# Attention scores and recurrence gates: pairs of 64-row matmuls in place of stacked 128-row ones, in a hybrid decoder layer on one core

## The chip, the cores and the metric

The kernel runs on one core of a Trainium2 chip, as one launch. The metric is the time of an execution on the device in microseconds (us); lower is better. The core's engines work side by side, each through its own instructions in order: TensorE (PE, with its weight loads listed apart as PEld), VectorE (DVE), ScalarE (ACT), GpSimd (POOL) and SyncE (SP), which issues most transfers. They wait for one another through semaphores. Matrix products land in PSUM, in eight banks of 128 partitions by 512 floats; all else lies in SBUF.

## What is computed

One layer of a hybrid decoder over 16 learned meta tokens and 1024 tokens of width 1024, in float32. Cut to what matters here:

```python
u = rmsnorm(h)                       # 1040 x 1024
z = u @ w_in                         # -> q (8 heads of 64), k, v (2 heads of 64), x_rec, y_rec (512 each)
# sliding-window attention, blocks of 128 queries against their own and the previous block of keys
s = einsum("qd,sd->qs", q_block, keys_256) * 64 ** -0.5      # for each head
p = softmax over s and a sink of the head; o = p @ v
# recurrence on x = conv4(x_rec), gates from 8 blocks of 64 channels
r = sigmoid(x_block @ w_a[block] + b_a)
i = sigmoid(x_block @ w_x[block] + b_x)
a = exp(-8 * r * softplus(-lam));  h_t = a_t * h_(t-1) + sqrt(1 - a_t**2) * i_t * x_t
h += rmsnorm(concat(o, gelu(y_rec) * h_rec) @ w_out)
h += rmsnorm(relu(rmsnorm(h) @ w_ff1) ** 2 @ w_ff2)
```

The two contractions that the change touches, the scores and the gates, are over 64 values each.

## The kernel before, in words

**Precision.** Every product of float32 matrices is made of single-pass products of split operands: each operand is a high part (a rounded copy, type fp32r) and a low part (the rest). `mm3` (L123) adds three matmuls into one bank: high x high, high x low, low x high. `split` (L94) makes the parts: ACT casts (L96), DVE subtracts (L99). The one matmul operand is loaded into the array as weights, a row of the array for each value of the contraction; the other one streams past, a column for each result.

**Stages.** First the tokens are normed, transposed and split, in four pieces of 272 and 256 tokens; each piece is projected to k, v, the first pair of query heads and the first chunk of x_rec (L430 to L459). Then come eight rounds of attention: four pairs j of query heads (head j on the first key head, head j + 4 on the second), two halves of four query blocks each (L702 to L714). Each round calls `scores`, then `next_fill`, a projection of the next q, x_rec or y_rec piece that is given a late priority so that it fills gaps, and `attend` of the round before. Then the gates of four chunks of 128 channels (`gates`, L731), two more projections of y_rec, the recurrence (`decay`, `recur`, `rec_out`), the output projection and the feed-forward part. The order within each engine comes from a scheduler with its own estimates; `behind` (L106) and `chained` (L286) fix some orders by hand, and `lut` keeps ACT's table functions in the order of the program.

**Scores.** A head has 64 values, half of the array's rows. The kernel fills the other half with the low part: q[h] (L400) holds the high part of the head's queries in one half of its 128 partitions and the low part in the other, and khh[h] (L264) holds the high part of the keys in both. One matmul of q[h] with khh[h] gives (high + low) x high; a second one, with kl[h], whose other half is zero, gives high x low. So a score product takes two 128-row matmuls (L555 and L559). The sinks that build this, `sink_k` (L376) and `sink_q` (L404), take two ACT and two DVE instructions of 64 partitions each for every piece, and four transfers on POOL's queue copy the high keys to the other half (L462, and L463 for the meta keys in km). A round works head by head; for each head it fills two banks tagged "s" in turn, two blocks of queries each. ACT copies half of a bank (L573) and DVE overwrites what lies above the diagonal (L574).

**Gates.** A chunk has 128 channels, two blocks of 64. Their weights are put into graw as a block-diagonal 128x128 matrix on a zeroed tile (L717 to L724), so that one 128-row `mm3` computes one gate for both blocks. A chunk takes two gates, three pieces of 348 or 344 tokens and three matmuls each: 18, and 72 in all. Each result goes through a sigmoid (L745) into a tile whose 128 partitions are the chunk's channels, as the recurrence needs them.

Of the kernel before, what the change touches and what calls it, by code (L numbers as in the profile page):

```python
# [10 lines left out]
F32R = mybir.dt.float32r  # L11
AF = mybir.ActivationFunctionType
# [25 lines left out]
def hybrid_layer(  # L38
# [30 lines left out]
    def f32(ap):  # L69
        return ap.bitcast(F32)  # L70
# [189 lines left out]
    REAL2 = [(16, 512), (528, 512)]  # L260

    khh = [slot("b", [P, T], F32R) for _ in range(2)]  # L264
    kl = [slot("b", [P, T], F32R) for _ in range(2)]
    HALF = (slice(0, HD), slice(HD, P))
    for h in range(2):
        nc.gpsimd.memset(f32(kl[h][HALF[1 - h]]), 0.0)

    zero = slot("ws", [P, 512])  # L270
    nc.vector.memset(zero, 0.0)
    km = const.tile([P, 4, P], F32R, name="km")
    vm = const.tile([P, 2, P], F32R, name="vm")
    nc.vector.tensor_copy(km.rearrange("p a b -> p (a b)"), zero)

# [81 lines left out]
    for i, src in enumerate((conv_b, b_a, b_x, lru_lambda)):  # L357
        nc.sync.dma_start(prm_r[4 + i : 5 + i, :], src)


    vk = [slot("b", [P, 8, P], F32R) for _ in range(2)]
    vt = slot("c", [P, TT])


    def high_k(hh, src):
        return [nc.scalar.copy(hh[h][HALF[h]], src[HALF[h]]).ins for h in range(2)]

    def low_k(hh, lo, src):
        return [
            nc.vector.tensor_tensor(  # L370
                lo[h][HALF[h]], src[HALF[h]], f32(hh[h][HALF[h]]), op=ALU.subtract
            ).ins
            for h in range(2)
        ]

    def sink_k(acc, t0, n):  # L376
        o = NMETA if t0 == 0 else 0
        c = slice(t0 + o - NMETA, t0 - NMETA + n)
        parts = [([khh[0][:, c], khh[1][:, c]], [kl[0][:, c], kl[1][:, c]], acc[:, o:])]
        if o:  # L380
            m, mk = slice(0, NMETA), slice(P - NMETA, P)
            parts.append(
                ([km[:, 0, mk], km[:, 1, mk]], [km[:, 2, mk], km[:, 3, mk]], acc[:, m])
            )
        ops = [[], []]
        for hh, lo, src in parts:
            ops[0] += high_k(hh, src)
        for hh, lo, src in parts:
            ops[1] += low_k(hh, lo, src)
        if o:  # L390
            for e in range(2):
                for ins in ops[e]:
                    chained(e, ins)

    def sink_v(acc, t0, n):
# [4 lines left out]
    def new_q():  # L400

        q = pair("b", [P, T])

        def sink_q(acc, t0, n):  # L404
            c = slice(t0 - NMETA, t0 - NMETA + n)
            for h in range(2):
                r = HALF[h]
                nc.scalar.activation(q[h][r, c], acc[r], AF.Copy, scale=-(HD ** -0.5))
            for h in range(2):
                r, o = HALF[h], HALF[1 - h]  # L410
                nc.vector.scalar_tensor_tensor(
                    q[h][o, c], acc[r], -(HD ** -0.5), f32(q[h][r, c]),
                    op0=ALU.mult, op1=ALU.subtract,
                )

        return q, sink_q

# [12 lines left out]
    for b in range(4):  # L430
# [29 lines left out]
    for h in range(2):  # L460
        r, o, m = HALF[h], HALF[1 - h], slice(P - NMETA, P)
        nc.gpsimd.dma_start(f32(khh[h][o]), f32(khh[h][r]))  # L462
# [76 lines left out]
    def scores(j, half, q):  # L539

        sn = slot("c", [P, 2, 4, P + 1])
        negm = small.tile([P, 2, 4], F32, name="negm", tag="negm")
        den = small.tile([P, 2, 4], F32, name="den", tag="den")
        rden = small.tile([P, 2, 4], F32, name="rden", tag="rden")
        for h in range(2):
            nc.gpsimd.tensor_copy(
                sn[:, h, :, P], nsink[:, j + 4 * h : j + 4 * h + 1].to_broadcast([P, 4])
            )
        for h in range(2):
            for bp in range(2):  # L550
                sp_ = bank("s", (P, 2, 256))

                def qk(dst, b, hi, lo):
                    c = slice(b * P, (b + 1) * P)
                    nc.tensor.matmul(  # L555
                        dst, q[h][:, c], hi, start=True, stop=False,
                        skip_group_check=True,
                    )
                    nc.tensor.matmul(  # L559
                        dst, q[h][:, c], lo, start=False, stop=True,  # L560
                        skip_group_check=True,
                    )

                for i in range(2):
                    b = 4 * half + 2 * bp + i
                    if b == 0:
                        qk(sp_[:, i, 0:P], b, km[:, h, :], km[:, 2 + h, :])
                        qk(sp_[:, i, P:256], b, khh[h][:, 0:P], kl[h][:, 0:P])
                    else:
                        c = slice((b - 1) * P, (b + 1) * P)  # L570
                        qk(sp_[:, i, :], b, khh[h][:, c], kl[h][:, c])
                s_ = sn[:, h, 2 * bp : 2 * bp + 2, 0:P]
                nc.scalar.copy(s_, sp_[:, :, P:256])  # L573
                nc.vector.copy_predicated(  # L574
                    s_, above_i.rearrange("p (a b) -> p a b", a=1).to_broadcast([P, 2, P]),
                    sp_[:, :, 0:P],
                )
                if half == 0 and bp == 0:
                    w = slice(0, P - NMETA)
                    nc.vector.copy_predicated(sn[:, h, 0, w], above_i[:, w], far)  # L580
            nc.vector.tensor_reduce(
                negm[:, h, :], sn[:, h], axis=mybir.AxisListType.X, op=ALU.min
            )
# [68 lines left out]
            )  # L652
        xc[c] = y

    ys = [None] * NLRU

    def fill_q(j):
        def run(w):
# [11 lines left out]

    def fill_y(c):
        def run(w):
            y = slot("b" if c == 1 else "d", [P, T])

            def sink(acc, t0, n):
                nc.vector.tensor_copy(y[:, t0 - NMETA : t0 - NMETA + n], acc)

            project(w, REAL2, sink)
            ys[c] = y
        return run  # L680
# [22 lines left out]
    for j in range(NPAIR):  # L703
        for half in range(2):
            if j % 2 == 0 and half == 0:
                at_pair(j // 2)
            sn = scores(j, half, qs[j])
            if True:
                with deferred(FILL_LAG):
                    next_fill()  # L710
            if prev is not None:
                attend(*prev)
            prev = (j, half, sn)
    attend(*prev)  # L714


    graw = slot("e", [P, 2, NLRU, P])  # L717
    behind(last_pow[0], nc.gpsimd.memset(graw, 0.0).ins)
    for i, w in enumerate((w_a, w_x)):
        for s in range(2):  # L720
            r = slice(HD * s, HD * s + HD)
            nc.sync.dma_start(
                graw[r, i, :, r], w[0, s::2].rearrange("n c d -> c n d")
            )  # L724
    gh = slot("e", [P, 2, NLRU, P], F32R)
    gl = slot("b", [P, 2, NLRU, P], F32R)
    split(gh, gl, graw)

    rg = [None] * NLRU

    def gates(c):  # L731
        ch, cl = pair("b", [P, TT])
        split(ch, cl, xc[c])
        rg[c] = []
        for i in range(2):
            t_ = slot("c", [P, TT])
            for t0, n in ((0, 348), (348, 348), (696, 344)):
                flip[0] += 1
                acc = bank(("s", "pt", "o")[flip[0] % 3])
                mm3(  # L740
                    acc[:, :n], (gh[:, i, c, :], gl[:, i, c, :]),
                    (ch[:, t0 : t0 + n], cl[:, t0 : t0 + n]), True, True,
                )
                lut(
                    t_[:, t0 : t0 + n], acc[:, :n], AF.Sigmoid,  # L745
                    bias=prm[:, c, 5 + i : 6 + i],
                )
            rg[c].append(t_)
        nc.vector.tensor_tensor(t_, t_, xc[c], op=ALU.mult)

    av = [None] * NLRU

# [4 lines left out]
        lut(r, r, AF.Tanh, scale=m4sp[:, c : c + 1])  # L757

    def recur(c):
        r, gi = rg[c]  # L760
        lut(r, r, AF.Sqrt, scale=-1.0)
        nc.vector.scalar_tensor_tensor(r, av[c], 1.0, r, op0=ALU.add, op1=ALU.mult)
        nc.vector.tensor_tensor(gi, gi, r, op=ALU.mult)
# [640 lines left out]
```

## Time and profile before

| | us |
|---|---|
| median of 3 runs (lowest, highest) | 969.04 (965.6, 969.07) |
| the profiled execution, its own time | 966.98 |
| its span, first to last instruction | 965.3 |

The granted TensorE clock of that execution was 0.998 of full. By stages, in us from the start of the span:

| stage | from | to | matmuls |
|---|---|---|---|
| loads, norm, first piece | 0 | 22 | 80 |
| other pieces of k, v, first q and x_rec | 22 | 62 | 337 |
| attention and most filling projections | 62 | 201.5 | 953 |
| gates, with projections of y_rec among them | 201.5 | 220.4 | 106 |
| recurrence, beside the last projections and the output projection | 220.4 | 270 | 214 |
| rest of the output projection, feed-forward | 270 | 965.3 | 3036 |

How to read the rows below. A row of a group gives its line, engine and operation, the tile written and those read, and the shape. A row of the timeline gives start and duration in us. Matmuls are pipelined: the end of one is modelled, and what counts is how far their starts stand apart. "64x512" on ACT or DVE means 64 partitions with 512 values each; the time goes with the 512. In the list of waits stand the engine and line that waited, who ended the wait, the total in us, the number of times, and the longest.

### The profile page before, as it was taken

How to read it: one execution, taken by the hardware profiler on the slowest of the kernel's cores; microseconds unless marked ns; L12 is line 12 of the kernel's file. 1: busy time of each engine (PE TensorE's matmuls, PEld its weight loads, DVE VectorE, ACT ScalarE, POOL GpSimd, SP SyncE). 2: the span in 40 equal slices, each digit the busy share in tenths (PEclk: the TensorE clock that was granted, in tenths of full speed). 3: DMA queues.
4: the chain of work that ended last, by engine and by line, in shares of the span. 5: the costliest groups of instructions: out<-in, count | busy, mean ns of one | idle time of the engine just before them, and what ended most of it. 6: DMA issues, size and time to landing. Idle time of an engine off the chain costs nothing.

```text
span 965.3 us, 12356 instructions
## 1 busy us (share of the span) xinstructions
PE 947.6 (98%) x4718; PEld 795.0 (82%) x4718; DVE 651.6 (68%) x833; ACT 503.2 (52%) x845; POOL 120.5 (12%) x183
## 2 busy tenths in 40 slices
PE   6999999999999999999999999999999999999996
PEld 6999999888878877888888888888888888888885
DVE  5567988856865695665654455468557676779884
ACT  6546765567744663443555566654433343436441
POOL 4202544500011100000000000000111100001201
PEclk9999999999999999999999999999999999999999
DMA  8121010013235457576423264324687765547934
GB/s 278 37 56 40 24 44 23 25 49 81 88 129 156 157 173 237 180 254 201 173 87 106 92 202 130 103 91 122 163 186 183 193 210 206 184 144 195 240 66 88
DMA packets 88155, 130.14 MB, mean 135 GB/s; under 512 B 13688, under 2 KB 52616, under 8 KB 88096
## 3 DMA queue, kind: packets, MB, share of 16 engines
q1 hardware_dynamic: 79504, 106.54, 34.0%
q0 software_dynamic: 8160, 21.51, 10.8%
q10 hardware_dynamic: 432, 1.31, 0.4%
q8 instruction: 37, 0.61, 0.3%
q14 instruction: 22, 0.18, 0.1%
HBM read 109.93 MB, written 18.87 MB: 133 GB/s over the span
## 4 chain that ended last, share of the span: by engine, by line
PE 81%; DVE 8%; ACT 4%; issue 3%; DMA 3%; POOL 1%; SPq 0%; DVEq 0%; ACTq 0%; POOLq 0%
PE ps_acc L125 9%; PE ps_acc L127 9%; PE ps_acc L126 9%; PE ps_pt L125 6%; PE ps_pt L127 5%; PE ps_pt L126 5%; PE ps_s L127 5%; PE ps_s L125 5%; PE ps_s L126 5%; PE ps_o L125 5%; PE ps_o L126 5%; PE ps_o L127 5%; ACT c L82 1%; PE ps_acc L253 1%; PE ps_o L620 1%
## 5 line engine op out<-in xcount | busy, mean ns | idle before, releaser
L96 ACT CAST ws<-raw 128x1024 fp32r<-128x1024 f32 (+1 forms) x68 | 69.6, 1024 | 120.7 <-PE ps_o L126 50.5
L99 DVE TENSOR_TENSOR ws<-raw,ws 128x1024 fp32r<-128x1024 f32 (+1 forms) x69 | 82.3, 1193 | 46.0 <-ACT ws L96 45.9
L125 PE MATMUL ps_acc<-a,ws 128*128 128x256 f32 (+2 forms) x256 | 85.8, 335 | 0.1
L126 PE MATMUL ps_acc<-a,ws 128*128 128x256 f32 (+2 forms) x256 | 85.4, 334 | 0.0
L127 PE MATMUL ps_acc<-a,ws 128*128 128x256 f32 (+2 forms) x256 | 84.9, 332 | 0.0
L99 DVE TENSOR_TENSOR b<-b,b 128x1024 fp32r<-128x1024 f32 (+2 forms) x48 | 57.5, 1199 | 32.3 <-PE ps_o L126 19.4
L96 ACT CAST ws<-e 128x1024 fp32r<-128x1024 f32 x41 | 42.9, 1045 | 65.4 <-PE ps_o L126 45.9
L96 ACT CAST b<-b 128x1024 fp32r<-128x1024 f32 (+2 forms) x47 | 48.8, 1037 | 37.3 <-DVE b L905 37.3
L99 DVE TENSOR_TENSOR ws<-e,ws 128x1024 fp32r<-128x1024 f32 x41 | 50.1, 1222 | 19.6 <-ACT ws L96 19.6
L609 POOL TENSOR_SCALAR_AFFINE_SELECT c<-c 128x512 fp32r<-128x512 f32 x64 | 52.6, 837 | 71.8 <-ACT c L96 61.9
L125 PEld LDWEIGHTS ps_acc<-a,ws 128*128 128x128 f32 x256 | 48.2, 188 | 4.6 <-ACT c L396 0.4
L127 PEld LDWEIGHTS ps_acc<-a,ws 128*128 128x128 f32 x256 | 48.2, 188 | 4.3
L126 PEld LDWEIGHTS ps_acc<-a,ws 128*128 128x128 f32 x256 | 48.2, 188 | 4.0
L125 PE MATMUL ps_acc<-ws,b 128*128 128x512 f32 (+1 forms) x120 | 46.2, 386 | 0.0
L127 PE MATMUL ps_acc<-ws,b 128*128 128x512 f32 (+1 forms) x120 | 46.2, 385 | 0.0
L126 PE MATMUL ps_acc<-ws,b 128*128 128x512 f32 (+1 forms) x120 | 46.1, 384 | 0.0
L125 PE MATMUL ps_pt<-ws,b 128*128 128x512 f32 x112 | 44.3, 395 | 0.0
L126 PE MATMUL ps_pt<-ws,b 128*128 128x512 f32 x112 | 44.1, 394 | 0.0
L127 PE MATMUL ps_pt<-ws,b 128*128 128x512 f32 x112 | 44.0, 393 | 0.0
L125 PE MATMUL ps_s<-ws,b 128*128 128x512 f32 x110 | 43.5, 395 | 0.0
L127 PE MATMUL ps_s<-ws,b 128*128 128x512 f32 x110 | 43.4, 394 | 0.0
L126 PE MATMUL ps_s<-ws,b 128*128 128x512 f32 x110 | 43.3, 394 | 0.0
(394 smaller groups left out, 2658.9 us busy)
## 6 DMA issues: line engine op xcount, KB each, us to landing
raw<-in_w_ff_dram SPq DMA_DIRECT2D x61, 512.0 KB, 3.8
e<-in_w_ff_dram SPq DMA_DIRECT2D x45, 512.0 KB, 3.8
d<-in_w_ff_dram SPq DMA_DIRECT2D x12, 512.0 KB, 3.8
s_dram<-d POOLq DMA_DIRECT2D x12, 512.0 KB, 4.0
raw<-in_w_in_dram SPq DMA_DIRECT2D x9, 512.0 KB, 4.6
c<-in_x_dram SPq DMA_DIRECT2D x8, 512.0 KB, 9.1
d<-in_x_dram SPq DMA_DIRECT2D x8, 512.0 KB, 4.8
out_dram<-raw SPq DMA_DIRECT2D x8, 512.0 KB, 2.6
```

The source lines that it names most:

```text
L82: ins = nc.scalar.activation(*args, **kwargs).ins
L96: nc.scalar.copy(hi, src)
L99: low = nc.vector.tensor_tensor(lo, src, f32(hi), op=ALU.subtract).ins
L125: nc.tensor.matmul(dst, lh, rh, start=start, stop=False, skip_group_check=True)
L126: nc.tensor.matmul(dst, lh, rl, start=False, stop=False, skip_group_check=True)
L127: last_mm[0] = nc.tensor.matmul(dst, ll, rh, start=False, stop=stop, skip_group_check=True).ins.name
L253: last_mm[0] = nc.tensor.matmul(acc[:, :n], w[k // 2][:, kc, :], u[kc][k % 2][:, t0 : t0 + n], start=k == 0 and kc == 0, stop=k == last an ...
L609: nc.gpsimd.affine_select(out=p_[:, :, s], in_=f32(p_[:, :, 0]), pattern=[[0, 4], [g, P]], compare_op=op, fill=0.0, base=0, channel_multip ...
L620: nc.tensor.matmul(po[:, oc : oc + n], v, p_[:, pc : pc + n], start=first and k == 0, stop=last and k == 1, skip_group_check=True,)
```

## The change

**Scores.** Queries and keys are no longer stacked. q[0] holds the high parts of both heads' queries, one head in each half of the partitions, and q[1] the low parts; kx[0] and kx[1] hold the keys in the same way. A score product is three matmuls of 64 rows, and head 0 uses the upper half of the array's rows while head 1 uses the lower half. The program writes the two heads' matmuls in turn, into two banks, one for each head. The second copies of the keys, their zeroed halves and the four transfers are gone; km has two columns of blocks in place of four. A sink now takes one ACT and one DVE instruction of 128 partitions. The softmax work is as before, but the banks of both heads are emptied after a group of 12 matmuls.

**Gates.** graw holds, for each block, its 64 rows with the columns of both gates side by side (64 + 64), without zeros. A matmul of 64 rows then gives both gates of one block: gate r in the first 64 partitions, gate i in the others. The two blocks of a chunk are written in turn, into two banks. Again 18 matmuls for each chunk. After the sigmoids, three transfers on POOL's queue, 64x1040 each, bring the halves together as the recurrence needs them; the third overwrites what the first has read. The biases b_a and b_x are loaded in the matching order, by four loads in place of two. The multiplication of gate i with x (`scaled_x`) is ordered behind a copy of y_rec.

```diff
-    khh = [slot("b", [P, T], F32R) for _ in range(2)]
-    kl = [slot("b", [P, T], F32R) for _ in range(2)]
+    kx = pair("b", [P, T])
...
-            for h in range(2):
-                r = HALF[h]
-                nc.scalar.activation(q[h][r, c], acc[r], AF.Copy, scale=-(HD ** -0.5))
-            for h in range(2):
-                r, o = HALF[h], HALF[1 - h]
-                nc.vector.scalar_tensor_tensor(
-                    q[h][o, c], acc[r], -(HD ** -0.5), f32(q[h][r, c]),
-                    op0=ALU.mult, op1=ALU.subtract,
-                )
+            split_scaled(q[0][:, c], q[1][:, c], acc, -(HD ** -0.5))
...
-    for h in range(2):
-        r, o, m = HALF[h], HALF[1 - h], slice(P - NMETA, P)
-        nc.gpsimd.dma_start(f32(khh[h][o]), f32(khh[h][r]))
-        nc.gpsimd.dma_start(f32(km[o, h, m]), f32(km[r, h, m]))
...
+        for bp in range(2):
+            sp_ = [bank("s", (P, 2, 256)) for _ in range(2)]
+            for i in range(2):
+                b = 4 * half + 2 * bp + i
+                cq = slice(b * P, (b + 1) * P)
+                if b == 0:
+                    cols = [(slice(0, P), km, None), (slice(P, 256), kx, slice(0, P))]
+                else:
+                    cols = [(slice(0, 256), kx, slice((b - 1) * P, (b + 1) * P))]
+                for dst, k_, c in cols:
+                    for n, (x0, x1) in enumerate(((0, 0), (0, 1), (1, 0))):
+                        for h in range(2):
+                            r = HALF[h]
+                            key = km[r, x1, :] if k_ is km else kx[x1][r, c]
+                            nc.tensor.matmul(
+                                sp_[h][:, i, dst], q[x0][r, cq], key, start=n == 0,
+                                stop=n == 2, skip_group_check=True,
+                            )
...
-    graw = slot("e", [P, 2, NLRU, P])
-    behind(last_pow[0], nc.gpsimd.memset(graw, 0.0).ins)
+    graw = slot("e", [P, NLRU, P])
     for i, w in enumerate((w_a, w_x)):
         for s in range(2):
             nc.sync.dma_start(
+                graw[HALF[s], :, HD * i : HD * i + HD],
+                w[0, s::2].rearrange("n c d -> c n d"),
+            )
+    gw = slot("e", [P, 2, NLRU, P], F32R)
+    behind(gate_after, nc.scalar.copy(gw[:, 0], graw).ins)
+    nc.vector.tensor_tensor(gw[:, 1], graw, f32(gw[:, 0]), op=ALU.subtract)
...
+        z = [slot("c", [P, TT]) for _ in range(2)]
+        for t0, n in ((0, 348), (348, 348), (696, 344)):
+            acc = []
+            for s in range(2):
                 flip[0] += 1
+                acc.append(bank(("s", "pt", "o")[flip[0] % 3]))
+            for k, (a, b) in enumerate(((0, ch), (0, cl), (1, ch))):
+                for s in range(2):
+                    nc.tensor.matmul(
+                        acc[s][:, :n], gw[HALF[s], a, c, :], b[HALF[s], t0 : t0 + n],
+                        start=k == 0, stop=k == 2, skip_group_check=True,
+                    )
+            for s in range(2):
+                lut(
+                    z[s][:, t0 : t0 + n], acc[s][:, :n], AF.Sigmoid,
+                    bias=prm[:, c, 5 + s : 6 + s],
                 )
+        gi = f32(ch)
+        for s in range(2):
+            nc.gpsimd.dma_start(gi[HALF[s]], z[s][HALF[1]])
+        nc.gpsimd.dma_start(z[0][HALF[1]], z[1][HALF[0]])
+        rg[c] = *z, gi
+
+    def scaled_x(c):
+        return nc.vector.tensor_tensor(rg[c][1], rg[c][2], xc[c], op=ALU.mult).ins
...
     for c in range(NLRU):
         gates(c)
-    for _ in range(2):
+    for c in range(2, NLRU):
         next_fill()
+        for k in (0, 1) if c == 2 else (2, 3):
+            behind(y_copies[2], scaled_x(k))
```

More of the change, by code (lines that the diff above doesn't have):

```diff
@@ L356, in hybrid_layer @@
     nc.sync.dma_start(prm_r[0:4, :], conv_w[0])
-    for i, src in enumerate((conv_b, b_a, b_x, lru_lambda)):
-        nc.sync.dma_start(prm_r[4 + i : 5 + i, :], src)
+    for i, src in ((4, conv_b), (7, lru_lambda)):
+        nc.sync.dma_start(prm_r[i : i + 1, :], src)
+    for i, src in enumerate((b_a, b_x)):
+        for s in range(2):
+            nc.sync.dma_start(
+                prm_r[5 + s : 6 + s, :].rearrange("o (c t k) -> t o c k", t=2, k=HD)[i],
+                src.rearrange("o (c t k) -> t o c k", t=2, k=HD)[s],
+            )
     vk = [slot("b", [P, 8, P], F32R) for _ in range(2)]
     vt = slot("c", [P, TT])
[L365 to L374, printed above, removed]
     def sink_k(acc, t0, n):
@@ L378, in sink_k @@
         c = slice(t0 + o - NMETA, t0 - NMETA + n)
[L379 removed]
+        parts = [(kx[0][:, c], kx[1][:, c], acc[:, o:])]
         if o:
[L381 to L392 removed]
+            mk = slice(P - NMETA, P)
+            parts.append((km[:, 0, mk], km[:, 1, mk], acc[:, :NMETA]))
+        for e in range(2):
+            for hi, lo, src in parts:
+                if e == 0:
+                    ins = nc.scalar.copy(hi, src).ins
+                else:
+                    ins = nc.vector.tensor_tensor(lo, src, f32(hi), op=ALU.subtract).ins
+                if o:
                     chained(e, ins)
@@ L548, in scores @@
             )
[L549 to L571, printed above, removed]
+        for bp in range(2):
[5 more added lines that the diff above has]
+                    cols = [(slice(0, P), km, None), (slice(P, 256), kx, slice(0, P))]
+                else:
+                    cols = [(slice(0, 256), kx, slice((b - 1) * P, (b + 1) * P))]
[8 more added lines that the diff above has]
+                            )
+            for h in range(2):
                 s_ = sn[:, h, 2 * bp : 2 * bp + 2, 0:P]
-                nc.scalar.copy(s_, sp_[:, :, P:256])
+                nc.scalar.copy(s_, sp_[h][:, :, P:256])
                 nc.vector.copy_predicated(
                     s_, above_i.rearrange("p (a b) -> p a b", a=1).to_broadcast([P, 2, P]),
-                    sp_[:, :, 0:P],
+                    sp_[h][:, :, 0:P],
                 )
@@ L580, in scores @@
                     nc.vector.copy_predicated(sn[:, h, 0, w], above_i[:, w], far)
+        for h in range(2):
             nc.vector.tensor_reduce(
@@ L733, in gates @@
         split(ch, cl, xc[c])
[L734 to L737, printed above, removed]
+        z = [slot("c", [P, TT]) for _ in range(2)]
+        for t0, n in ((0, 348), (348, 348), (696, 344)):
+            acc = []
+            for s in range(2):
                 flip[0] += 1
[L739 to L742, printed above, removed]
-                )
[L744 to L749, printed above, removed]
+                acc.append(bank(("s", "pt", "o")[flip[0] % 3]))
[9 more added lines that the diff above has]
+                    bias=prm[:, c, 5 + s : 6 + s],
+                )
+        gi = f32(ch)
+        for s in range(2):
+            nc.gpsimd.dma_start(gi[HALF[s]], z[s][HALF[1]])
[3 more added lines that the diff above has]
+        return nc.vector.tensor_tensor(rg[c][1], rg[c][2], xc[c], op=ALU.mult).ins
     av = [None] * NLRU
```

22 lines of the change are left out of this document (8 added, 14 removed).

## The prediction

> **What bounds the kernel now.** I read the page first, then what TensorE waited for, then its load stage by stage, then its matmuls one by one.
>
> ```profile
> span 965.3 us, 12356 instructions
> ...
> PE 947.6 (98%) x4718; PEld 795.0 (82%) x4718; DVE 651.6 (68%) x833; ACT 503.2 (52%) x845; POOL 120.5 (12%) x183
> ...
> PE 81%; DVE 8%; ACT 4%; issue 3%; DMA 3%; POOL 1%; SPq 0%; DVEq 0%; ACTq 0%; POOLq 0%
> ```
>
> TensorE is busy for 98% of the span and holds 81% of the chain that ends last. A busy PE can still be a slow one, so the list of its waits counts for more:
>
> ```profile
> PE ps_s L306 <- DVE d L231: 6.1, 1, 6.1
> PE ps_acc L253 <- DVE km L370: 0.9, 1, 0.9
> ...
> PE ps_o L620 <- POOL c L609: 0.6, 1, 0.6
> PE ps_pt L125 <- ACT b L96: 0.2, 1, 0.2
> ```
>
> After the first 6.1 us it waits for nothing worth a microsecond. The table by stage says the same of the stretch that the change touches (columns: PE, PEld, DVE, ACT, POOL busy, clock):
>
> ```profile
> 22.00:62.00 40.00, 39.88 (x337) 39.45 (x338) 23.07 (x58) 21.27 (x52) 8.74 (x19) 1.00 0.15 35
> 62.00:201.50 139.50, 138.92 (x953) 128.13 (x952) 113.86 (x190) 84.29 (x247) 55.48 (x76) 1.00 0.16 42
> 201.50:220.40 18.90, 18.90 (x106) 17.48 (x105) 7.21 (x7) 13.98 (x26) 0.00 (x0) 1.00 0.12 29
> 220.40:270.00 49.60, 49.39 (x214) 39.55 (x212) 40.67 (x42) 36.55 (x42) 0.00 (x0) 1.00 0.28 85
> ```
>
> From 22 to 270 us PE idles 0.9 us in all, at full clock. So the change is worth what it does to PE's own time there, plus what it does to the few waits. ACT and DVE have slack and count only where such a wait ends on them.
>
> **The price of a matmul.** What counts is the distance between starts, since the ends overlap:
>
> ```profile
> 96.11 0.28 PE L555 MATMUL ps_s<-km,b 128*128 128x128 f32 x1
> 96.22 0.27 PE L559 MATMUL ps_s<-km,b 128*128 128x128 f32 x1
> 96.33 0.28 PE L555 MATMUL ps_s<-b,b 128*128 128x128 f32 x1
> ...
> 96.84 0.28 PE L555 MATMUL ps_s<-b,b 128*128 128x256 f32 x1
> 96.96 0.28 PE L559 MATMUL ps_s<-b,b 128*128 128x256 f32 x1
> 97.08 0.28 PE L555 MATMUL ps_s<-b,b 128*128 128x256 f32 x1
> ```
>
> A score matmul of 256 columns takes 0.118 us, one of 128 columns 0.11. The gates run 15 in a row between these two starts, (220.40 - 218.03) / 15 = 0.158 us each:
>
> ```profile
> 218.03 0.32 PE L125 MATMUL ps_pt<-b,e 128*128 128x348 f32 x1
> ...
> 220.40 0.40 PE L125 MATMUL ps_acc<-a,ws 128*128 128x512 f32 x1
> ```
>
> **Scores and gates before.** 8 rounds (4 q pairs, 2 halves), 2 heads, 4 blocks, 2 matmuls each; block 0 takes two column pieces. That is 112 x 0.118 + 32 x 0.11 = 16.7 us. Gates: 72 x 0.158 = 11.4 us.
>
> **After, if two row halves run side by side.** Nothing in this trace shows a pair, so the cost lies between one matmul's time and two. A 64-row matmul streams as many columns, so alone I price it as before. Scores need three products instead of two: 168 matmuls of 256 columns and 48 of 128. Gates stay at 72. A pair shares a slot only where a matmul of the other half stands next to it. In the order as the changed program is built this is not always so: many runs read AAABBBABABAB, not ABABAB. Going through that order, letting a matmul start with its predecessor if the half differs, I count 108 + 27 slots for scores and 44 for gates. Scores become 108 x 0.118 + 27 x 0.11 = 15.7 us (-1.0), gates 44 x 0.158 = 7.0 us (-4.4): together **-5.4**. If nothing overlaps: 168 x 0.118 + 48 x 0.11 = 25.1 us (+8.4), gates 0. I take the first: the two halves use other rows of the array and other PSUM banks.
>
> **The way in and out of 64 rows.** The trace has a near case, four transposes of 8 rows between full ones:
>
> ```profile
> 55.29 0.38 PE L306 MATMUL ps_s<-ident,d 128*128 128x128 f32 x2
> 55.60 0.41 PE L469 MATMUL ps_o<-ident,d 8*128 8x8 f32 x4
> 55.95 0.44 PE L528 MATMUL ps_pt<-ident,c 128*128 128x128 f32 x2
> ```
> ```profile
> 55.19 0.25 PEld L306 LDWEIGHTS ps_s<-ident,d 128*128 128x128 f32 x2
> 55.60 0.32 PEld L469 LDWEIGHTS ps_o<-ident,d 8*128 8x128 f32 x4 [0.17 <-issue]
> ```
>
> Full ones go 0.11 apart, the small ones 0.06 (0.32 less one load's 0.14, over three). From 55.29 to 55.95 two and four should take 0.46 us and took 0.66; no engine released the 55.60 load, the 0.17 before it is put to issue. So an excursion costs 0.20, and a little more until loads run ahead again: I take **0.22**, between 0.10 (one side only) and 0.35 (512-column matmuls around it). The built order has 24 excursions for scores and 4 for gates: 28 x 0.22 = **+6.2 us** (2.8 to 9.8). That eats the gain.
>
> The Trainium skill (TensorE: Matmul & The Clock Gate, section "LDWEIGHTS (loading the stationary operand)") says that a load's time follows its columns and not its rows. The rows differ: 8-row loads 0.06 apart, full ones 0.11. By the page a 64-row load costs as much as a full one, and the first rival below is what would follow; between those two rows the trace does not decide.
>
> **The sinks, and two waits.** Stacked halves took two instructions where one now does:
>
> ```profile
> L408 ACT ACTIVATE b<-ps_acc x20: 372/591/607, 25.0 to 156.2; 64x512 fp32r<-64x512 f32 x12, 64x256 fp32r<-64x256 f32 x8
> L411 DVE SCALAR_TENSOR_TENSOR b<-ps_acc,b x20: 418/684/694, 26.4 to 158.1; 64x512 fp32r<-64x512 f32 x12, 64x256 fp32r<-64x256 f32 x8
> L366 ACT CAST b<-ps_acc x8: 365/367/369, 19.4 to 60.5; 64x256 fp32r<-64x256 f32 x8
> L370 DVE TENSOR_TENSOR b<-ps_acc,b x8: 416/422/428, 20.6 to 61.3; 64x256 fp32r<-64x256 f32 x8
> ```
>
> Half of each go. Most of it is hidden under PE and worth nothing. The 0.9 us wait for L370 at the first key piece should go: one 0.37 cast and one 0.42 subtraction fewer stand before the bank is free, and the two of the meta columns (-0.9, at least 0). Late is then the next projection's own load, which is there. The wait at L620 hangs on ACT and DVE work in which the last query sink stands:
>
> ```profile
> 155.64 0.59 ACT b L408
> 156.24 0.59 ACT b L408
> ```
>
> One 0.59 goes from that chain: -0.6 (at least 0).
>
> **Both score banks at once.** Before, a head filled one bank while the other was emptied; now a group of 12 fills both and the next one waits for both.
>
> ```profile
> L573 ACT COPY c<-ps_s x32: 352/374/405, 70.0 to 171.6; 128x256 f32<-128x256 f32 x32
> L574 DVE COPY_PREDICATED c<-above,ps_s x32: 423/445/465, 71.8 to 172.5; 128x256 f32<-128x256 int32 x32
> ```
>
> Emptying two takes 2 x (0.37 + 0.45) = 1.6 us. The cover is at least 23 other matmuls between groups, 2.7 us at 0.118. If DVE is late it is gone; behind the waiting matmul stand all others. Eight of the fifteen gaps are that short, so at worst 8 x 0.82 = 6.6; I take one, +0.8.
>
> **Gate halves moved by DMA.** 12 transfers of 64x1040, three per chunk, the third behind the first; four of the old key copies go. The nearest transfer:
>
> ```profile
> L462 POOL DMA_DIRECT2D b<-b x2: 527/570/612, 60.7 to 61.4; - x2
> DMA to landing us min/median/max: 3.0/3.3/3.7
> ```
> ```profile
> 220.60 0.55 ACT L82 ACTIVATE c<-ps_o,prm 128x344 f32<-128x344 f32 x1
> 221.18 1.24 DVE L749 TENSOR_TENSOR c<-c,b 128x1040 f32<-128x1040 f32 x1 [3.61 <-ACT c L82]
> 229.50 2.40 DVE L762 SCALAR_TENSOR_TENSOR c<-b,c 128x1040 f32<-128x1040 f32 x2 [3.23 <-ACT c L82]
> ```
>
> POOL is idle there. The last chunk's multiplication, moved behind the copies of y, can run 2 x 3.3 us after 221.15, to 229.0 with its 1.24; the next on DVE in the built order is what is now L762, at 229.50. Just hidden; the chain behind it reaches PE with no slack (the 0.2 wait), so each microsecond late is lost. I take +0.2, 0 to 2. Two more small parameter loads stand on SP's queue; nothing in PE's list of waits hangs on a load there.
>
> **Sum.** -5.4 + 6.2 - 0.9 - 0.6 + 0.8 + 0.2 = +0.3 us. The profiled execution took 966.98 us (span 965.3 and 1.7 around it): **967.3**. The median of the runs, 969.04, lies 2 us above it.
>
> **Rivals.**
> 1. Loads go one at a time. For: full loads stand 0.11 apart even where 128 columns stream. Then every 64-row matmul costs 0.11: scores 216 x 0.11 = 23.8 (+7.1), gates 72 x 0.11 = 7.9 (-3.5), +6.2 - 0.5 for the rest: +9.3, **976.3**, slower. It decides once a load takes more than 0.059, half a slot. Against: the 8-row loads.
> 2. No overlap: +8.4 + 0 + 6.2 - 0.5 = +14.1, **981.1**. The change would then not do what it says; nothing in the trace speaks against it but the separate rows and banks.
> 3. Changing to 64 rows stalls nothing: -5.4 - 0.5 = -5.9, **961.1**. Against: 55.29 to 55.95.
>
> **How the numbers follow.** Forecast 0.50, rival 1 0.18, rival 2 0.18, rival 3 0.14. The forecast's own range is 963 to 975 (excursions from 2.8 to 9.8, plus some of the late banks); of its 0.50 I put 0.04 over 0.5% faster (4.8 us, about what a measurement of this kernel can tell from no change), 0.12 over 0.5% slower. Faster 0.14 + 0.04 = 0.18; slower 0.18 + 0.18 + 0.12 = 0.48; same 0.34. The range 961.1 to 981.1 leaves out half of rivals 2 and 3, 0.16.
>
> **What would show it.** Starts of an A and a B matmul nearly together show the overlap; 0.11 between them shows loads in a row, 0.118 to 0.158 none. About 0.2 us more than usual where 128 and 64 rows meet shows the excursion, nothing there rival 3. The gates with their y matmuls, 18.9 us now, should shrink to 18.9 - 11.4 + 7.0 + 4 x 0.22 = 15.4. Waits of PE for DVE or ACT at the new score line, or at the first gate chunk's DVE work, would show the banks or DMAs mis-sized. Wrong altogether would be a PE that idles for microseconds between 62 and 270 us.

## The result and the profile after

The changed kernel took 971.47 us (median of 7 runs, 970.14 to 972.95) against 967.28 us for the kernel before (7 runs, 965.6 to 969.07): a ratio of 1.0046 (95% interval 1.0032 to 1.0059), 4.2 us slower. The forecast was 967.3, no change. The profiled execution took 972.28 us; its span is 4.9 us longer than before's.

From the page of the changed kernel, the span, the busy times, and the chain that ended last by engine:

```profile
span 970.2 us, 12466 instructions
...
PE 949.6 (98%) x4790; PEld 788.3 (81%) x4790; DVE 640.1 (66%) x818; ACT 495.0 (51%) x830; POOL 111.7 (12%) x188
...
PE 93%; DMA 2%; DVE 2%; issue 2%; POOL 1%; ACT 0%; SPq 0%; DVEq 0%; POOLq 0%; ACTq 0%
```

PE is busy for 2 us more and the span is 4.9 us longer: part of the loss is slower work, part is idle time. The list of what PE waited for tells which idle time is new:

```profile
PE ps_s L302 <- DVE d L231: 5.8, 1, 5.8
PE ps_pt L126 <- DVE a L99: 2.1, 2, 1.3
PE ps_pt L125 <- DVE ws L98: 1.4, 1, 1.4
...
PE ps_o L592 <- POOL c L581: 0.2, 1, 0.2
```

The wait at the first key piece (0.9 before) is gone, and that at the attention's second matmul, L592 here, is 0.2 (0.6 before). New are 3.5 us at L125 and L126 for DVE: these are the first matmuls of the output projection, behind the gates. At L538, the new score line, PE waits for no engine. The table by stage (PE, PEld, DVE, ACT, POOL busy, clock, DMA share, GB/s) puts the idle time in one place:

```profile
62.00:206.20 144.20, 144.02 (x1023) 126.81 (x1020) 108.30 (x195) 81.05 (x241) 46.63 (x77) 1.00 0.14 38
206.20:220.80 14.60, 14.60 (x106) 11.62 (x105) 4.79 (x5) 11.14 (x22) 3.75 (x7) 1.00 0.41 92
220.80:275.00 54.20, 50.64 (x218) 40.00 (x215) 43.47 (x45) 37.78 (x45) 2.64 (x6) 1.00 0.50 132
```

By the starts of the first and last matmul of each kind, three stages changed:

| stage | before | after | difference |
|---|---|---|---|
| last matmul of the first piece to first gate matmul (attention) | 173.2 | 178.2 | +5.0 |
| first to last gate matmul | 18.65 | 14.5 | -4.2 |
| last gate matmul to first transposition after the output projection | 71.0 | 74.9 | +3.9 |

The attention lost 5.0 us with 0.2 us of idle time: PE ran on, but more slowly. The gates gained 4.2 as hoped. Then 3.6 us of idle time (54.20 less 50.64; 0.2 in the same stage before) and the restarts behind it gave back 3.9.

**How a run of 64-row matmuls looks.** The gates of the last chunk, by PE's starts; below, their loads:

```profile
219.04 0.39 PE L127 MATMUL ps_acc<-a,ws 128*128 128x512 f32 x1
219.36 0.43 PE L717 MATMUL ps_s<-b,e 64*128 64x348 f32 x1
219.37 0.43 PE L717 MATMUL ps_pt<-b,e 64*128 64x348 f32 x1
219.63 0.32 PE L717 MATMUL ps_s<-b,e 64*128 64x348 f32 x1
219.64 0.32 PE L717 MATMUL ps_pt<-b,e 64*128 64x348 f32 x1
219.79 0.32 PE L717 MATMUL ps_s<-b,e 64*128 64x348 f32 x1
219.80 0.32 PE L717 MATMUL ps_pt<-b,e 64*128 64x348 f32 x1
...
220.74 0.32 PE L717 MATMUL ps_o<-b,e 64*128 64x344 f32 x1
220.99 0.50 PE L125 MATMUL ps_acc<-a,ws 128*128 128x512 f32 x1
221.33 0.39 PE L126 MATMUL ps_acc<-a,ws 128*128 128x512 f32 x1
221.56 0.39 PE L127 MATMUL ps_acc<-a,ws 128*128 128x512 f32 x1
```
```profile
219.63 0.18 PEld L717 LDWEIGHTS ps_s<-b,e 64*128 64x128 f32 x1
219.64 0.18 PEld L717 LDWEIGHTS ps_pt<-b,e 64*128 64x128 f32 x1
```

Two matmuls of different halves start 0.01 us apart, pairs 0.16 apart, and the two loads of a pair 0.01 apart. So the halves do run side by side, loads too. The edges cost: a 512-column matmul takes 0.23, yet 219.04 to 219.36 is 0.32 (+0.09); the first pair takes 0.27 in place of 0.16 (+0.11); 220.74 to 220.99 is 0.25 in place of 0.16 (+0.09); 220.99 to 221.33 is 0.34 in place of 0.23 (+0.11). Together **0.40 us** for one excursion. A group of scores between 256-column matmuls tells the same:

```profile
173.26 0.28 PE L126 MATMUL ps_acc<-a,ws 128*128 128x256 f32 x1
173.47 0.98 PE L538 MATMUL ps_s<-b,b 64*128 64x256 f32 x12
174.38 0.39 PE L127 MATMUL ps_acc<-a,ws 128*128 128x256 f32 x1
174.61 0.28 PE L125 MATMUL ps_acc<-a,ws 128*128 128x256 f32 x1
```

From 173.26 to 174.61 stand one matmul, six pairs and one matmul: 8 x 0.118 = 0.94 us, and it took 1.35: 0.41 more.

**Where the idle time comes from.** POOL's transfers (L729 a chunk's first two, L730 its third), the time to landing of those of L729, DVE's work in that stretch, and PE's idle time:

```profile
220.39 1.02 POOL L729 DMA_DIRECT2D b<-c  x2
226.49 0.51 POOL L730 DMA_DIRECT2D c<-c  x1 [5.09 <-DMA b<-c]
227.02 1.02 POOL L729 DMA_DIRECT2D b<-c  x2
231.65 0.51 POOL L730 DMA_DIRECT2D c<-c  x1 [3.61 <-DMA b<-c]
```
```profile
DMA to landing us min/median/max: 3.3/4.3/7.5
```
```profile
229.67 1.24 DVE L734 TENSOR_TENSOR c<-b,d 128x1040 f32<-128x1040 f32 x1 [5.55 <-DMA c<-c]
230.83 0.69 DVE L98 CAST ws<-raw 128x1024 fp32r<-128x1024 f32 x1
...
234.58 1.24 DVE L734 TENSOR_TENSOR c<-b,b 128x1040 f32<-128x1040 f32 x1 [1.33 <-DMA c<-c]
235.74 1.23 DVE L747 SCALAR_TENSOR_TENSOR c<-b,c 128x1040 f32<-128x1040 f32 x1
```
```profile
229.84 0.40 PE L127 MATMUL ps_acc<-a,ws 128*128 128x512 f32 x1
231.67 0.47 PE L125 MATMUL ps_pt<-ws,b 128*128 128x512 f32 x1 [1.43 <-DVE ws L98]
```

The third transfer of a chunk waits on POOL's queue until the first has landed, and behind it wait the next chunk's first two: chunk 3's (the last one's) start at 227.02, though its last gate matmul ran at 220.74. DVE's `scaled_x` of chunk 2 writes over the tile that the third transfer reads, so it waits for that landing too, until 229.67. Behind it on DVE stands the cast of the first w_out weights (L98, 230.83), and for that one PE waits at 231.67. Chunk 2's first two transfers are also the slowest, 5.6 and 7.5 us to landing against 3.3 to 4.6 for the other chunks'. SyncE issues two loads of w_out at the same moment (220.39 and 220.90), which is the likely reason, but not tested by itself. PE's idle microseconds between 62 and 270 us are what the prediction had named as a sign of being wrong altogether.

### The profile page after: what moved, and what is told of

Read it like the earlier page. It is cut to its first block, busy times and chain, and to the rows that moved or that the text cites. A ratio compares the mean times of both kernels' runs of the same rounds, so it can differ in the third digit from the quotient of the medians.

```text
span 970.2 us, 12466 instructions
## 1 busy us (share of the span) xinstructions
PE 949.6 (98%) x4790; PEld 788.3 (81%) x4790; DVE 640.1 (66%) x818; ACT 495.0 (51%) x830; POOL 111.7 (12%) x188
## 4 chain that ended last, share of the span: by engine, by line
PE 93%; DMA 2%; DVE 2%; issue 2%; POOL 1%; ACT 0%; SPq 0%; DVEq 0%; POOLq 0%; ACTq 0%
PE ps_acc L125 11%; PE ps_acc L126 11%; PE ps_acc L127 10%; PE ps_pt L126 6%; PE ps_s L127 6%; PE ps_pt L127 6%; PE ps_pt L125 6%; PE ps_s L125 6%; PE ps_s L126 6%; PE ps_o L126 5%; PE ps_o L127 5%; PE ps_o L125 5%; PE ps_o L592 2%; PE ps_s L538 2%; PE ps_acc L253 1%
## 5 line engine op out<-in xcount | busy, mean ns | idle before, releaser
L125 PE MATMUL ps_acc<-a,ws 128*128 128x256 f32 (+2 forms) x256 | 86.5, 338 | 0.0
L126 PE MATMUL ps_acc<-a,ws 128*128 128x256 f32 (+2 forms) x256 | 86.0, 336 | 0.0
L581 POOL TENSOR_SCALAR_AFFINE_SELECT c<-c 128x512 fp32r<-128x512 f32 x64 | 44.4, 719 | 84.8 <-ACT c L96 81.2
L125 PEld LDWEIGHTS ps_acc<-a,ws 128*128 128x128 f32 x256 | 48.3, 189 | 5.7 <-issue 0.4
L126 PEld LDWEIGHTS ps_acc<-a,ws 128*128 128x128 f32 x256 | 48.2, 188 | 5.2 <-issue 0.4
L126 PE MATMUL ps_acc<-ws,b 128*128 128x512 f32 (+1 forms) x120 | 46.2, 385 | 1.0 <-DVE ws L99 1.0
L125 PE MATMUL ps_acc<-ws,b 128*128 128x512 f32 (+1 forms) x120 | 46.2, 386 | 0.0
L125 PE MATMUL ps_pt<-ws,b 128*128 128x512 f32 x112 | 44.4, 396 | 1.4 <-DVE ws L98 1.4
L126 PE MATMUL ps_pt<-ws,b 128*128 128x512 f32 x112 | 44.0, 393 | 0.0
L125 PE MATMUL ps_s<-ws,b 128*128 128x512 f32 x110 | 43.4, 395 | 0.0
L126 PE MATMUL ps_s<-ws,b 128*128 128x512 f32 x110 | 43.3, 394 | 0.0
```

Of the source, the lines that this page charges most:

```text
L125: nc.tensor.matmul(dst, lh, rh, start=start, stop=False, skip_group_check=True)
L126: nc.tensor.matmul(dst, lh, rl, start=False, stop=False, skip_group_check=True)
L581: nc.gpsimd.affine_select(out=p_[:, :, s], in_=f32(p_[:, :, 0]), pattern=[[0, 4], [g, P]], compare_op=op, fill=0.0, base=0, channel_multip ...
```

## The experiments

The theory after the result had two parts: each excursion into 64 rows costs more than forecast, and the gates' transfers, by their order and their landings one behind the other, give back what the gates gain. The expectations' figure of 0.286 us counts an excursion's two edges and the reload behind it, but not the 0.11 of the first pair.

**1. Each part alone.** scores_only has the changed scores, queries and keys with the gates of before:

```diff
-    khh = [slot("b", [P, T], F32R) for _ in range(2)]
-    kl = [slot("b", [P, T], F32R) for _ in range(2)]
+    kx = pair("b", [P, T])
...
+                                sp_[h][:, i, dst], q[x0][r, cq], key, start=n == 0,
```

> The changed scores, queries and keys, with the gates as before. Theory (28 changes into 64 rows at 0.286 us each, read from the trace after, and gate transfers that block one another): the scores carry 24 of the 28, 6.9 us, less 1.0 us of slots and 1.5 us of sinks and waits, so about 4.4 us slower than before, and no idle time of PE at the score lines. Rival (the loss is all behind the gates, the scores come out near even as forecast): within 1.5 us of before.

Measured: 969.29 us against 967.04, ratio 1.0022 (1.0008 to 1.0035), +2.2 us: slower, but less than the theory gave and, by the median, more than the rival. By the stages of its trace the attention lasts 177.8 us, 4.6 more than before's, as expected, and PE waits for no engine from 27 to 270 us. So the part that the change touches costs what the theory says. The total is less sure. The traced execution took 971.73 us, 2.4 above the median. Its first 28 us are 1.7 shorter than in before's trace, a stretch in which traces without the changed sinks (before, gates_only, gates_sp, gates_swap) differ by 1.4. What follows the output projection is 1.8 us longer, and there the traces of all kernels differ by up to 3.4 us, with the same code.

gates_only has the changed gates with the scores, queries and keys of before:

```diff
-    gh = slot("e", [P, 2, NLRU, P], F32R)
-    gl = slot("b", [P, 2, NLRU, P], F32R)
+    gw = slot("e", [P, 2, NLRU, P], F32R)
...
+        for s in range(2):
+            nc.gpsimd.dma_start(gi[HALF[s]], z[s][HALF[1]])
+        nc.gpsimd.dma_start(z[0][HALF[1]], z[1][HALF[0]])
```

> The changed gates with the scores, queries and keys as before. Theory: the gate matmuls give 11.4 - 6.2 us less 4 x 0.286 = 4.1 us, and the three transfers of each chunk, in order on one queue, give 3.9 of it back: about 0.2 us faster than before, with the same idle times of PE for DVE and ACT at the output projection. Rival (the two waits appear only because the scores moved the rest about): about 4 us faster than before.

Measured: 967.19 us, ratio 1.0005 (0.9995 to 1.0016), no difference. The gates last 14.5 us here too, and the stretch behind them 75.6 in place of 71.0: all given back. So the waits belong to the gates' part, not to the shifted scores. Alone the two parts make +2.2 and +0.2 us by the medians, less than the changed kernel's 4.2; each has an interval of 1 us and more to either side, and where the rest belongs is not settled. One idle stretch was longer than in the changed kernel, and that had a price of its own (PE's rows, then the table of the stretch with the clock behind POOL's busy time; the row at 226.27 names ACT, but the operand ws is that of L98, whose cast on DVE ended at 226.13):

```profile
223.86 0.40 PE L127 MATMUL ps_acc<-a,ws 128*128 128x512 f32 x1
226.27 0.47 PE L125 MATMUL ps_pt<-ws,b 128*128 128x512 f32 x1 [2.01 <-ACT c L82]
...
228.61 0.63 PE L127 MATMUL ps_acc<-a,ws 128*128 128x512 f32 x1
229.04 0.63 PE L125 MATMUL ps_acc<-a,ws 128*128 128x512 f32 x1
```
```profile
226.00:228.00 2.00, 1.69 (x5) 1.22 (x6) 1.86 (x3) 1.97 (x3) 0.51 (x1) 0.84 0.35 83
228.00:230.00 2.00, 2.00 (x6) 1.52 (x6) 0.65 (x1) 2.00 (x5) 0.00 (x0) 0.50 0.75 155
230.00:232.00 2.00, 2.00 (x9) 1.59 (x8) 2.00 (x3) 0.69 (x1) 0.00 (x0) 0.81 1.07 254
```

After 2.01 us of idle time the granted clock falls to half, some 1.1 us after PE has started again, and 512-column matmuls stand 0.43 apart in place of 0.23. Lost are 2 x (0.16 + 0.50 + 0.19) = 1.7 us beside the waits of 2.0 and 0.8.

**2. The price of an excursion.** extra128 adds one 128-row matmul to each score group, extra64 the same with 64 rows; the added result is overwritten:

```diff
+                if i == 1:
+                    nc.tensor.matmul(
+                        sp_[0][:, 1, :], q[0][0:P, cq], kx[0][0:P, cols[0][2]],
+                        start=True, stop=True, skip_group_check=True,
+                    )
```

(extra64 has 0:HD in place of 0:P.)

> The changed kernel with one more matmul of 128 rows and 256 columns in each of the 16 score groups, before its second block; its result is overwritten. It cuts the run of 64-row matmuls in two, so that PE's order has 40 excursions into 64 rows and not 28. To be compared with extra64, which has 25. Theory (0.286 us for each excursion, whatever stands around it): 15 x 0.286 = 4.3 us slower than extra64. Rival (the lost time at the scores is a wait for banks or a load that happens to stand there): within 1 us of extra64.

> The control: the same additional matmul with 64 rows in place of 128, so that the run of 64-row matmuls isn't cut; 25 excursions. Either theory: 16 matmuls of 256 columns at no more than 0.118 us, 1 to 2 us slower than the changed kernel, less three excursions under the theory (-0.9).

Measured: 978.45 us (ratio 1.0114, 1.0101 to 1.0127) and 972.39 us (1.0054, 1.0042 to 1.0066), 6.1 us apart. That rules the rival out. The stretch of the score matmuls, by the first and last starts of their line, in extra64 and then in extra128:

```profile
L543 PE MATMUL ps_s<-b,b x192: 270/277/387, 67.9 to 174.5; 64*128 64x256 f32 x168, 64*128 64x128 f32 x24
L543 PE MATMUL ps_s<-km,b x24: 268/274/327, 61.3 to 156.8; 64*128 64x128 f32 x24
```
```profile
L543 PE MATMUL ps_s<-b,b x192: 269/277/391, 67.7 to 181.1; 64*128 64x256 f32 x168, 64*128 64x128 f32 x24
L543 PE MATMUL ps_s<-km,b x24: 269/274/327, 61.1 to 161.8; 64*128 64x128 f32 x24
```

From the first km score to the last b score: 113.2 and 120.0 us. If the added matmul costs as much in either, about 16 x 0.118, that is 6.8 / 15 = 0.45 us for each excursion by the trace, 0.40 by the medians, and not the 0.286 that I had expected: the first pair's delay belongs to it. The kernel extra64 itself is 0.8 us over the changed kernel by their ratios, within the 0.1 to 1.1 that the expectation comes to with its three excursions fewer.

**3. The transfers.** gates_sp moves only each chunk's third transfer from POOL's queue to SyncE's; after_sp does the same in the changed kernel:

```diff
-        nc.gpsimd.dma_start(z[0][HALF[1]], z[1][HALF[0]])
+        nc.sync.dma_start(z[0][HALF[1]], z[1][HALF[0]])
```

> As gates_only, but the third transfer of each chunk goes to SyncE's queue, so that it no longer holds back the next chunk's first two. Theory (head-of-line order on POOL's queue): DVE's wait for the last chunk falls from 5.5 us to under 1, the waits of PE at the output projection go, 3 to 4 us faster than before. Rival (the 3.3 us landings themselves, or the recurrence's own chain on DVE and ACT, set the time): as gates_only, within 1 us of before.

> The changed kernel with the third transfer of each chunk on SyncE's queue. Theory: 3.5 to 4 us faster than the changed kernel, so within 1 us of before (+0.3): the changes into 64 rows remain. Rival (landings or the chain set the time): as the changed kernel, 4 to 5 us slower than before.

Measured: gates_sp 965.07 us, ratio 0.9976 (0.9967 to 0.9985), 2.0 us faster than before; after_sp 967.75 us, 1.0012 (1.0000 to 1.0024), some 3.5 us faster than the changed kernel. So order on the queue counts, but gates_sp gained half of what the theory gave. DVE still waits, now for a third transfer that lands late:

```profile
223.99 1.24 DVE L769 TENSOR_TENSOR c<-b,d 128x1040 f32<-128x1040 f32 x1 [5.16 <-DMA c<-c]
225.15 0.69 DVE L98 CAST ws<-raw 128x1024 fp32r<-128x1024 f32 x1
```
```profile
PE ps_pt L125 <- DVE ws L98: 1.6, 1, 1.6
```

Two landings one behind the other still stand ahead of `scaled_x`, and L98 behind it; PE waits 1.6 us for L98. Either the chain of landings, or the number of bytes, was left.

**4. Two that failed by a side effect.** gates_inplace lets `scaled_x` write over the moved gate i, which needs a tile of its own; gates_two also drops the transfer that moved a half to the partitions where it already was:

```diff
-        gi = f32(ch)
+        gi = slot("b", [P, TT])
...
-        return nc.vector.tensor_tensor(rg[c][1], rg[c][2], xc[c], op=ALU.mult).ins
+        return nc.vector.tensor_tensor(rg[c][2], rg[c][2], xc[c], op=ALU.mult).ins
```

(gates_two has two instructions of 64 partitions there, one `dma_start` fewer, and the cross transfer of gate r on SyncE's queue.)

> As gates_only, but the multiplication of gate i with x writes over the moved gate i, in a tile of its own, and no longer over the tile that the third transfer reads. All three transfers stay on POOL's queue. Theory A (DVE waits for the third transfer only because it overwrites what that one reads): DVE's waits at this line shrink by one landing of 2.9 us for each of the last two chunks, 1.5 to 2.5 us faster than gates_only. Theory B (order on POOL's queue decides): the last chunk's first two transfers still start 15 us late, under 1 us faster than gates_only. Theory C (the sixteen DMA engines are full): as B.

> As gates_inplace with two transfers for each chunk: the second one moved a half to the partitions where it already was, and here DVE multiplies the two halves by themselves (one instruction more for each chunk). The other cross transfer goes to SyncE's queue. Theories A and B together with C (a third of 3.2 MB fewer): DVE waits under 1.5 us in all for the gates' transfers, PE's waits at the output projection go, 3 to 4 us faster than before. Rival (DVE and ACT's own recurrence chain sets the output projection's start): no more than gates_sp's 2 us.

Measured: 970.9 us (1.0041, 1.0029 to 1.0053) and 968.24 us (1.0016, 1.0007 to 1.0026), both slower than before, which no theory had. They tell nothing of the transfers, because the new tile changed something else. What PE waited for among the gates, in gates_inplace:

```profile
PE ps_s L752 <- ACT b L96: 3.2, 1, 3.2
```

ACT's cast of the last chunk's x came to stand behind the third chunk's sigmoids, with no projection in PE's order to fill the time. PE idled 3.2 us, then ran at half clock until about 227. gates_two shows the same wait.

**5. No transfer behind another's landing.** gates_swap exchanges the two gates' columns in the second block. Then gate r is in place in both blocks; two independent transfers cross gate i over, and POOL copies one half of r within its partitions:

```diff
-                graw[HALF[s], :, HD * i : HD * i + HD],
+                graw[HALF[s], :, HD * (i ^ s) : HD * (i ^ s) + HD],
...
-            nc.gpsimd.dma_start(gi[HALF[s]], z[s][HALF[1]])
-        nc.gpsimd.dma_start(z[0][HALF[1]], z[1][HALF[0]])
+            nc.sync.dma_start(gi[HALF[s]], z[s][HALF[1 - s]])
+        nc.gpsimd.tensor_copy(z[0][HALF[1]], z[1][HALF[1]])
```

(The loads of the biases change in the same way.) It stands on before's scores; after_swap has it in the changed kernel.

> The changed gates, with the scores, queries and keys as before, and the columns of the second block's two gates exchanged. Then gate r lies where it is needed in both blocks; two transfers on SyncE's queue, independent of each other, cross gate i over, and POOL copies one half of r in place. No transfer waits for another's landing. Theory (the transfers' chain and order gave back the gates' gain): DVE waits for them under 2 us in all, PE's waits at the output projection and the half-clock stretch of gates_only are gone, 3 to 4 us faster than before. Rival (the recurrence's chain on DVE and ACT sets the output projection's start): PE still waits 2 us or more there, at most 2 us faster than before.

> The changed kernel with the gates of gates_swap. Theory: what the transfers gave back is gone, so it is 3.5 to 4.5 us faster than the changed kernel and equal to before within 1 us; what is left of the scores' 24 excursions (6.9 us) is just paid by the gates. Rival: within 1.5 us of the changed kernel.

Measured: gates_swap **962.67 us, ratio 0.9962 (0.9950 to 0.9974), 4.0 us faster than before**, the best of all. after_swap 968.19 us, 1.0016 (1.0007 to 1.0025): 3.3 us faster than the changed kernel by medians, 1.6 slower than before, a little outside what I expected. In gates_swap PE's idle time behind the gates is down to 0.9 us, at full clock:

```profile
199.00:215.00 16.00, 16.00 (x111) 12.39 (x110) 6.06 (x6) 11.59 (x23) 2.34 (x2) 1.00 0.37 89
215.00:270.00 55.00, 54.10 (x233) 43.27 (x233) 44.15 (x46) 40.06 (x51) 2.67 (x3) 1.00 0.42 119
```
```profile
219.81 1.24 DVE L769 TENSOR_TENSOR c<-b,d 128x1040 f32<-128x1040 f32 x1 [5.53 <-DMA b<-c]
220.97 0.69 DVE L98 CAST ws<-raw 128x1024 fp32r<-128x1024 f32 x1
```
```profile
223.85 0.40 PE L125 MATMUL ps_pt<-ws,b 128*128 128x512 f32 x1
```

I had expected DVE's wait to shrink below 2 us. It did not: it is 5.5 us. But it ends at 219.81, 4.2 us earlier than in gates_sp, so that L98 is done at 221.7 and PE, which comes to it at 223.85, finds it there. What counts is the end of a wait against its deadline, not its length.

By the ratios gates_swap is only 1.4 us ahead of gates_sp, and their intervals overlap. The stage from the last gate matmul to the first transposition after the output projection tells them apart: 75.6 us in gates_only, 73.8 in gates_sp, 71.8 in gates_swap, 71.0 before. In the changed kernel it goes the same way, 74.9, then 73.1 in after_sp and 71.8 in after_swap, although after_swap as a whole is no faster than after_sp (1.0016 and 1.0012).

gates_swap has also fewer bytes. gates_swap3 adds a third transfer of the same size, to DRAM, that nothing in the chain waits for:

```diff
+        nc.sync.dma_start(spare[c], z[0][HALF[0]])
```

> As gates_swap, with a third transfer of the same size for each chunk that nothing in the chain waits for: it writes one half of gate r to a spare place in DRAM. So the bytes are those of the changed kernel's gates, but no transfer waits for another's landing. Theory B (each third transfer stood behind the landing of the first, and held the queue): as gates_swap, 3.5 to 4 us faster than before. Theory C (3.2 MB were too much for the sixteen DMA engines in that time): DVE's wait for the last chunk grows by about the 1.2 us that 0.27 MB take at 220 GB/s for each chunk still under way, PE waits at the output projection again, 1 to 2.5 us faster than before.

Measured: 962.6 us, 0.9962 (0.9948 to 0.9975), as gates_swap; L98 starts at 221.47. With 3.2 MB the time is the same, so the bytes were not the matter. That leaves the landings one behind the other, together with the queue that they held. Not separated is how much of gates_swap's gain over gates_sp comes from SyncE's queue in place of POOL's for the first two transfers. Not tried was holding the w_out loads back until chunk 2's transfers have landed.

## Why the prediction was wrong

By its own steps:

| step | predicted | measured |
|---|---|---|
| score matmuls (16.7 before) | -1.0 | about -4.2 |
| gate matmuls (11.4 before) | -4.4 | about -5.7 |
| 28 excursions into 64 rows | +6.2 | about +11.2 |
| sinks: wait for L370, wait at L620 | -1.5 | about -0.8 |
| both score banks at once | +0.8 | 0 |
| gate halves moved by DMA | +0.2 | +3.9 |
| sum | +0.3 | about +4.4 (medians +4.2, spans +4.9) |

- **The halves run side by side** was right, and rivals 1 and 2 fell: starts 0.01 us apart, for matmuls and for loads. Rival 3 fell by the edges. The slots were mis-sized. I counted in the order as built, where a run of AAABBB shares few slots. On the chip the last chunk's first six matmuls, AAABBB in the built program, start in pairs. So scores take 84 x 0.118 + 24 x 0.11 = 12.5 us and gates 36 x 0.158 = 5.7. That a load's time follows its columns and not its rows (the Trainium skill, TensorE: Matmul & The Clock Gate, section "LDWEIGHTS (loading the stationary operand)") did not bring rival 1: two 64-row loads share their time. A 64-row load of 128 columns lasts 0.18 us here and a 128-row one 0.19, so the trace agrees with the Trainium skill there.
- **The way in and out of 64 rows** was the right mechanism at half its size: 0.22 us predicted, 0.40 measured on the rows above, 0.40 to 0.45 by extra128 against extra64. The four 8-row transposes did not show the first pair's delay, and little of the reload behind it. I gave 0.35 as the upper end; it was too low. These two errors nearly cancel: -9.9 + 11.2 = +1.3 in place of -5.4 + 6.2 = +0.8.
- **Sinks and two waits**: the two waits fell from 0.9 and 0.6 us to none and 0.2. But the 0.9 stood before the last matmul of the first piece, and that stretch takes 27.1 us on average in the six traces with the changed sinks and 27.6 in the seven without. So about 0.4 of the 0.9 came through, in a stretch that differs by more than that from trace to trace.
- **Both score banks at once** cost nothing: PE waits for no engine at L538, so the 23 matmuls between groups were cover enough.
- **Gate halves moved by DMA is the step that failed.** I let only the last chunk's two landings of 3.3 us count, "just hidden" before 229.50, and put the step at +0.2. It cost 3.9. Left out were the other chunks: their third transfers hold POOL's queue, so that the last chunk's first two start 6 us after its last gate matmul, and landings under load took up to 7.5 us. Left out was also what stands behind `scaled_x` on DVE: not only L747 but L98, the cast of the first w_out weights, which PE reaches first. It was chunk 2's `scaled_x`, not the last chunk's, that held L98. The text had the rule (each microsecond late is lost) and the bound of 2 us, but not the queue. gates_swap, which takes that away, is 4.0 us faster than before, and the changed kernel with it gets 3.3 us back.
- **The sign**: the stage of the gates was forecast at 15.4 us with its edges and took 14.5. The 971.5 us lie within the 963 to 975 of the forecast, but that is luck: its upper part stood for dearer excursions and late banks, while faster matmuls paid for the excursions, the banks cost nothing, and the time was lost at the transfers. The forecast's "no change" rested on +0.2 for them.

## What to carry to other kernels

Count an excursion into 64-row matmuls on TensorE as a fixed price for each run, 0.40 us here, and ask how long the runs are: 18 gate matmuls that save 1.4 us (5.7 in four runs) pay it, a group of 12 score matmuls that saves 0.26 (4.2 in sixteen, which the built order cuts into 24 runs) does not. When results land in the wrong partitions, lay out the weights so that as little as possible has to cross, and let no transfer wait for another's landing on a queue that the next chunk needs. A wait is priced by what stands behind it on its engine and by when PE comes for that.

## What the runs showed of the hardware

- PE does not keep to the built order between the halves: matmuls that stand as AAABBB in the built program, three of one row half and three of the other, started in pairs (219.36 and 219.37, 219.63 and 219.64, 219.79 and 219.80).
- An idle PE costs more than its idle time once the clock falls. After 1.4 us (changed kernel) and 1.6 us (gates_sp) the granted clock stayed at 1.00; after 2.0 us (gates_only) it fell to 0.50 for 3.4 us, a loss of 1.7, after 3.2 us (gates_inplace and gates_two) for 6.8. Where between 1.6 and 2.0 us the limit lies, or whether it is a fixed one, is not shown. The Trainium skill (TensorE: Matmul & The Clock Gate, section "HAM oscillation — how this bites in real kernels") names idle gaps of more than about 3.4 us as those to avoid; here 2.0 us was enough.
- A chunk's first two transfers of 64x1040 land in 3.3 and 3.6 us when little else is under way (the changed kernel's first chunk) and in 5.6 and 7.5 us with two w_out loads issued beside them (its third chunk), at up to 230 GB/s in stretches of 2 us.
